# A decoder layer on one core: gate matrices stored in three pieces, and two small loads issued by GpSimd instead of SyncE

## The chip, the cores and the metric

The kernel runs on one core of a Trainium2 chip. The time is device microseconds (us) of one execution, lower is better. The engines are called as the profile calls them: PE (TensorE; PEld is its weight load), DVE (VectorE), ACT (ScalarE), POOL (GpSimd) and SP (SyncE, which only issues DMAs). DMAs issued by SP run on queue q1, those issued by ACT on q10, those issued by POOL on q0; all run on the same 16 DMA engines.

## The reference

One layer on 512 tokens of width 1024: a mixer (Mamba-2 heads beside latent attention), a LayerNorm, and a PEER channel mixer, followed by a last LayerNorm. The change lies in the PEER part, which is, cut to what matters:

```python
q = (xb @ w_query).reshape(T, 8, 2, 128)
s = einsum('thkd,hknd->thkn', q, sub_keys)          # 2 x 128 scores per head
sv, si = top_k(s, 16)
cand_s = sv[:, :, 0, :, None] + sv[:, :, 1, None, :]
top_s, top_pos = top_k(cand_s, 16)                  # 8 heads x 16 experts of 16384
gate = softmax(top_s)
u = take(u_table, expert_idx)                       # rows of 1024
act = gelu(einsum('td,thkd->thk', xb, u))
v = take(v_table, expert_idx)
out = einsum('thk,thkd->td', gate * act, v)
```

## The kernel before, in words

**Tokens.** The 512 tokens are four blocks of 128. Tokens 0 to 335 (`NU`) are done densely: PE multiplies them with the whole table `u` (128 chunks of 128 experts, `u_chunk`), and later a gate-weighted matrix `P` with the whole table `v`. The 48 tokens after them (`UG`, the last of block 2) get their products with `u` by gathering rows (`ug_dots`), and block 3 does both tables by gathering (`gather`).

**Table loads.** `Stream` brings each 512 KB chunk of a table. `loads` issues the load on SP into one of three `wir` buffers (L104), `his` makes the rounded copy `wih` on ACT (L122; every fourth is called `wihx`), `splits` makes the remainder `wil` on DVE, or on POOL while `lo_on` is POOL (L132). A load waits until the subtraction has freed its buffer. A chunk `u_half` is three matmuls for each of eight slices (L85 to L87), and `act_gelu` on ACT empties the accumulator `pu` (L1410, L1411); there are two accumulators.

**Order.** Each engine works through its own list in the order in which the program was written. `drive` interleaves table chunks with another piece of work by estimated durations. After the query projection and the top-16 selection (POOL does the subtractions there) comes `stage2`, which decodes the selected experts of blocks 0 to 2 on DVE (L1054 to L1102); inside it, `ug_index` computes the row numbers of the 48 tokens and sends them by POOL through memory (`ugi`, L1134; `uix`, L1137), and `ug_fetch` gathers rows (`urow`, L1154).

**The inputs of the gathered products.** `UR["x"]` are two tiles in columns of `XT` that are no longer needed. They hold the activations of the 48 tokens, each repeated over partitions: the first has 32 tokens four times, the second 16 tokens eight times (`SETS`). Between the top-16 selection and `stage2` SP loads each with one DMA (L1518), whose source repeats through a step of zero, and whose rows are cut in 16 runs of 64 numbers (256 bytes) by the shape of the tile.

**Gate matrices.** `build_g` then makes, in 48 groups (`n`), the dense gate matrix of blocks 0 to 2. A group is 16 small matmuls (L1291, L1292) and two copies by ACT into `stg` (L1294). Four groups fill one `stg` tile (two alternate), whose store to `gsp[k]` in HBM is one DMA on ACT's queue after the fourth (L1302; L1305 for the last two). Beside this run table chunks, the row gathers and their products (L1160), and, when the buffers for activations are full, stores of activations (`asp<-aout`, L1428, on SP). Then comes the long stage on table `v`, from about 830 us on.

Of the kernel before, what the change touches and what calls it, by code (L numbers as in the profile page):

```python
# [24 lines left out]
D = 1024  # L25
# [6 lines left out]
UG = 48  # L32
SETS = ((16, 32), (0, 16))
NU = NT - UG
ND = NU // 32
NA = ND * 32 + 32
FIRST = 40
KEEP = 51
MORE = 12
# [27 lines left out]
def tile_block(ctx: ExitStack, tc: tile.TileContext, I, out):  # L67
    nc = tc.nc
    ctx.enter_context(tc.manual_schedule())
    V, A, T, G = nc.vector, nc.scalar, nc.tensor, nc.gpsimd  # L70
# [3 lines left out]
    def pool(name, bufs=1, **kw):  # L74
        p = tc.alloc_tile_pool(name=name, bufs=bufs, **kw)
        opened.append(p)
        return p
# [151 lines left out]
    xsp = dram.tile([NB, 128, D], F32, name="xsp")  # L229
    gs0 = dram.tile([128, 2, NT // 32 - ND, 128], F32, name="gs0")  # L230
    gsp = dram.tile([NT // 32, 128, 128, 32], F32, name="gsp")
    acd = dram.tile([64, 128], F32, name="acd")
    ugi = dram.tile([UG, 128], I32, name="ugi")
    asp = dram.tile([PRE - KEEP, 128, NA], F32, name="asp")
    ugg = dram.tile([UG, 128], F32, name="ugg")
# [455 lines left out]
    for n in range(8):  # L691
# [4 lines left out]
        for kk in range(2):  # L696
            k = kp * 2 + kk
# [249 lines left out]
    wide = lambda z: z.rearrange("p (a b) -> p a b", b=64)  # L947
    scl = xt.tile([128, 1], F32, name="scl")
    xt.tile([128, 64], F32, name="edge")
    one16 = xt.tile([128, NA - NU], F32, name="one16")  # L950
    V.memset(one16, 1.0)
# [161 lines left out]
    late = []  # L1113
# [12 lines left out]
    GT, UR = {}, {}  # L1126
    done = []
# [80 lines left out]
    def digits():  # L1208
        dT = ijp.tile([128, 2, 64, 2], F16, name="dT")
        i = GT["ps"][0][:, 2]  # L1210
        x = B1.rearrange("p a b c -> p (a b c)").bitcast(F32)[:, :128].rearrange("p (k c) -> p k c", c=2)
        V.tensor_scalar(x, i, -3.5, BIG, op0=OP.add, op1=OP.add)
        V.tensor_scalar(dT[:, 0], x, -BIG, None, op0=OP.add)
        V.tensor_tensor(dT[:, 1], i, dT[:, 0], op=OP.subtract)
        GT["d"] = dT
# [11 lines left out]
    def build_g():  # L1227
        AT = gb.tile([128, 32, 16, 2], F16, name="tens")
        BT = gb.tile([128, 32, 16, 2], F16, name="units")

        def half(n):
            k0 = n % 16 * 4
            for z, it, w, e in ((AT, iotaE[:, 0:128:8], 16, 0), (B1, iotaE[:, 0:8], 8, 1)):
                b = [128, 32, w, 2]
                V.tensor_tensor(z, it[:, None].to_broadcast(b),
                                GT["d"][:, e, k0:k0 + 32, None].to_broadcast(b), op=OP.is_equal)

        def gates(n, m):
            k = slice(n % 8 * 4, n % 8 * 4 + (m - n) * 4)
            b = [128, (m - n) * 4, 2, 8, 2]  # L1240
            gT = GT[n // 16][1][:, n % 16 * 4:n % 16 * 4 + (m - n) * 4]
            V.tensor_tensor(BT[:, k].rearrange("p k (e i) c -> p k e i c", e=2), B1[:, k, None].to_broadcast(b),
                            gT[:, :, :, None].to_broadcast(b), op=OP.mult)

        def hot(n):
            jT, _, rT = GT[n // 16]
            m = n % 16
            oj = gb.tile([128, 4, 128, 2], F16, name="oj", bufs=2)
            b2 = [128, 4, 128, 2]
            V.tensor_tensor(oj, iotaE[:, None].to_broadcast(b2),  # L1250
                            jT[:, m * 4:m * 4 + 4, None].to_broadcast(b2), op=OP.is_equal)
            g = gb.tile([128, 4, 16, 16, 2], F16, name="g", bufs=2)
            w = 8 if n in LOWA else 16
            b4 = [128, 4, 16, w, 2]
            k = slice(n % 8 * 4, n % 8 * 4 + 4)
            V.tensor_tensor(g[:, :, :, :w], AT[:, k, :, None].to_broadcast(b4),
                            BT[:, k, None, :w].to_broadcast(b4), op=OP.mult)
            for t in range(8 if n in LOWA else 0):
                q, c = divmod(t, 2)
                A.activation(g[:, q, :, 8:, c], g[:, q, :, :8, c], AF.Copy, scale=rT[:, m // 2, q, c:c + 1])  # L1260
            return oj, g

        late = []
        digits()
        g_low()
        half(0)
        gates(0, 8)
        nxt = hot(0)
        dots, head = UR["dots"], ug_head()
        tm[1] += 7.5  # L1270
        yield 2.6
        for n in range(48):
            b, g = divmod(n, 16)
            oj, og = nxt
            lump = 0.0
            if n < 47:
                m = n + 1
                if m % 8 == 0 or m == GG:
                    gates(m, GG if m // 8 == GG // 8 and m < GG else m // 8 * 8 + 8)
                    lump += 0.7  # L1280
                nxt = hot(m)
                if m % 8 == 7 and m < 47:
                    half(m + 1)
                    lump += 1.15
            if g % 4 == 0:
                stg = gs[(n // 4 + 1) % 2].tile([128, 128, 32], F32, name="stg")
            for hf in range(2):
                ps = pw()
                for t in range(4):
                    q, c = hf * 2 + t // 2, t % 2  # L1290
                    T.matmul(ps[:, t * 128:(t + 1) * 128], oj[:, q, :, c], og[:, q, :, :8, c], start=True, stop=False)  # L1291
                    T.matmul(ps[:, t * 128:(t + 1) * 128], oj[:, q, :, c], og[:, q, :, 8:, c], start=False, stop=True)  # L1292
                q0 = g % 4 * 8 + hf * 4
                A.activation(stg[:, :, q0:q0 + 4],  # L1294
                             ps.rearrange("p (t i) -> p i t", t=4), AF.Copy, scale=1.0 / GSC)
            tm[0] += 1.2
            if g % 4 == 3:
                k = n // 4
                if k < ND:
                    done.append(min(FIRST, (un[0] - 2) // 4 * 4))  # L1300
                    late.append((n + 2, k, stg))
                    nc.scalar.dma_start(gsp[k][:, done[k]:], stg[:, done[k]:])  # L1302
                else:
                    nc.scalar.dma_start(gs0[:, :, k - ND], stg[:, 0:8].rearrange("j (q i) t -> j q (i t)", q=2))
                    nc.scalar.dma_start(gsp[k][:, 8:], stg[:, 8:])  # L1305
            if late and late[0][0] <= n:
                _, k, z = late.pop(0)
                acts = ALL[0][:, :done[k], k * 32:k * 32 + 32]
                V.tensor_tensor(acts, acts, z[:, :done[k]], op=OP.mult)
                lump += 0.15 + done[k] * 0.034  # L1310
            if b < 2:
                if g == 9:
                    g_head(b + 1)
                if g == 11:
                    digits()
                    lump += 0.9
                if g == 12:
                    g_low()
                    lump += 1.1
            for _ in range(1 + n % 2):  # L1320
                tm[1] += next(dots, 0.0)
            if 36 <= n <= 40:
                tm[1] += next(head)
            yield lump + (1.45 if n + 1 in LOWA else 1.95) if n < 47 else 0.1
# [43 lines left out]
    aps = [pool("act")]  # L1368
    ALL = [aps[0].tile([128, FIRST, NA], F32, name="acts")]
    out_ = pool("aout")  # L1370
# [7 lines left out]
    def act_tile():  # L1378
# [5 lines left out]
        an[0] += 1  # L1384
        if n < FIRST:
            return ALL[0][:, n]
        return aps[k].tile([128, NA], F32, name="act", bufs=sizes[k] - (0 if k else FIRST))

    def end_tile():
        while an[0] % LEAD < FIRST:  # L1390
            an[0] += 1
        return act_tile().bitcast(F32R)
# [16 lines left out]
    def act_gelu(t, ps):  # L1409
        A.activation(t[:, :NU], ps, AF.Gelu)  # L1410
        A.activation(t[:, NU:], one16, AF.Copy)  # L1411

    def u_half(c, e, psum=None):
# [5 lines left out]
        if e:  # L1419
# [5 lines left out]
            else:  # L1425
                t = out_.tile([128, NA], F32, name="aout", bufs=2)
                act_gelu(t, ps)
# [79 lines left out]
    ug = pool("ug")  # L1507
    UR["x"] = spare(384), spare(448)
    UR["x3"] = UR["x"][0]
    UR["ix"] = ijp.tile([128, UG], I32, name="uix")  # L1510
    UR["hd"] = ijp.tile([128, UG], F32, name="uhd")
    UR["g"] = ijp.tile([UG, 128], F32, name="ugw")
    rt2 = pool("rt2")
    iaE = rt2.tile([128, 16, 16], F16, name="iaE")
    nc.sync.dma_start(iaE.rearrange("p a b -> p (a b)"), I["ch"][:, 256:512])
    for (r, z), x in zip(SETS, UR["x"]):
        d = xsp[2, 128 - UG + r:128 - UG + r + z]
        nc.sync.dma_start(x, bass.AP(tensor=d.tensor, offset=d.offset, ap=[[0, 128 // z], [D, z], [64, 16], [1, 64]]))  # L1518
    lo_on[0] = V
    drive(stage2())  # L1520
    close(rt2)
# [5 lines left out]
    B1 = gb.tile([128, 32, 8, 2], F16, name="unit")  # L1527
    least[0] = 1
    drive(build_g())
    close(gb, *gs)  # L1530
    GS = [-1, 0, 0]
# [91 lines left out]
    def v_prep(c):  # L1623
# [11 lines left out]
        if nb < ND:  # L1635
            A.activation(P[:, nb * 32:ND * 32], a[:, nb * 32:ND * 32], AF.Copy)
        A.activation(P[:, NA:], gt[c // 4][:, ND + 1, c % 4, :], AF.Copy)
        if c % 4 == 3:
# [237 lines left out]
```

## Time and profile before

| | |
|---|---|
| three runs | 1587.13, 1587.03, 1580.26 us |
| median | 1587.03 us |
| profiled execution, its own time | 1587.41 us |
| its span, first to last instruction | 1585.6 us |
| mean granted clock of PE | 0.995 |
| busy in the span: PE, DVE, ACT, POOL | 1552.5, 1345.8, 768.0, 619.2 us |
| moved by DMA | 406.52 MB |

The span is what the profile's rows are counted in; 1.8 us of the execution lie around it. Times at the left of a row are us from the span's start. A row in brackets tells how long the engine stood idle before the instruction and what ended that. A `q` behind an engine's name is its queue, where DMAs are issued.

### The profile page before, as it was taken

What the parts mean: (1) busy time and instruction counts of PE and PEld (TensorE: products, weight loads), DVE (VectorE), ACT (ScalarE), POOL (GpSimd) and SP (SyncE); (2) the same over time, 40 slices, a digit from 0 to 9 for tenths busy, and PEclk for the clock granted to TensorE, in tenths of its full rate; (3) what the DMA queues carried; (4) which work ended last, traced back from release to release, by engine and by line L of the source; (5) the groups of instructions that cost most, each with busy time, mean ns of one, the idle gap of its engine ahead of it and who ended that gap; (6) DMA issues with size and microseconds to landing.
All of it is one profiled execution on the core that took longest, in us unless ns stands there. A gap on an engine that the chain in (4) does not pass through costs nothing.

```text
span 1585.6 us, 24470 instructions
## 1 busy us (share of the span) xinstructions
PE 1552.5 (98%) x8696; PEld 1362.6 (86%) x8696; DVE 1345.8 (85%) x2643; ACT 768.0 (48%) x1539; POOL 619.2 (39%) x443
## 2 busy tenths in 40 slices
PE   9999999999999899999999999999999999999997
PEld 7887888888888899999898999999988878888886
DVE  8978767647799989899976888888889989889997
ACT  5565476731433447676765444443433334344442
POOL 0000032600244224343114655665555556667720
PEclk9999999999999999999999999999999999999999
DMA  6242122474423568899878999999999999999994
GB/s 251 94 160 91 47 75 62 131 236 140 130 81 100 139 220 293 328 337 324 275 249 310 345 360 351 368 355 363 372 336 365 358 360 363 368 341 358 358 314 145
DMA packets 150375, 406.52 MB, mean 256 GB/s; under 512 B 17812, under 2 KB 58980, under 8 KB 148460
## 3 DMA queue, kind: packets, MB, share of 16 engines
q1 hardware_dynamic: 98188, 209.16, 39.2%
q0 software_dynamic: 49648, 176.07, 30.4%
q10 hardware_dynamic: 2416, 19.73, 3.2%
q8 instruction: 68, 1.11, 0.3%
q14 instruction: 55, 0.45, 0.1%
HBM read 374.16 MB, written 28.65 MB: 254 GB/s over the span
## 4 chain that ended last, share of the span: by engine, by line
PE 76%; DMA 8%; DVE 8%; ACT 4%; issue 3%; POOL 0%; DVEq 0%; ACTq 0%; SPq 0%; POOLq 0%
PE va L1677 9%; PE va L1673 9%; PE va L1674 9%; PE pu L85 8%; PE pu L87 8%; PE pu L86 8%; DMA wir<-v 4%; PE pa L86 3%; PE pa L85 3%; PE pa L87 3%; PE pw L86 3%; PE pw L87 3%; PE pw L85 3%; DVE wil L132 2%; DMA wir<-ut 2%
## 5 line engine op out<-in xcount | busy, mean ns | idle before, releaser
L122 ACT ACTIVATE wih<-wir 128x1024 fp32r<-128x1024 f32 (+2 forms) x269 | 277.5, 1032 | 264.7 <-DMA wir<-v 173.7
L132 DVE TENSOR_TENSOR wil<-wir,wih 128x1024 fp32r<-128x1024 f32 (+1 forms) x234 | 282.7, 1210 | 84.3 <-ACT wih L122 59.2
L87 PE MATMUL pu<-XT,wil 128*128 128x336 f32 x1008 | 320.0, 317 | 4.7 <-DVE wil L132 4.3
L1674 PE MATMUL va<-wil,Ph 128*128 128x512 f32 x726 | 282.7, 389 | 0.0
L1554 POOL DMA_INDIRECT row<-v,ix x128 | 222.4, 1738 | 133.3 <-DVE ac L1571 108.7
L1673 PE MATMUL va<-wih,Ph 128*128 128x512 f32 x624 | 243.4, 390 | 0.0
L1554 POOL DMA_INDIRECT row<-u,ix x128 | 187.2, 1463 | 134.2 <-DVE row L1565 97.6
L85 PE MATMUL pu<-XT,wih 128*128 128x336 f32 x648 | 208.0, 321 | 1.0 <-ACT acts L1410 1.0
L86 PE MATMUL pu<-XT,wih 128*128 128x336 f32 x648 | 204.8, 316 | 0.0
L87 PEld LDWEIGHTS pu<-XT,wil 128*128 128x128 f32 x1008 | 190.5, 189 | 6.2 <-DVE wil L132 5.4
L1677 PE MATMUL va<-wih,Pl 128*128 128x512 f32 x624 | 192.9, 390 | 1.1 <-DVE Pl L1664 1.1
L1571 DVE SCALAR_TENSOR_TENSOR ac<-row,hd,ac 128x1024 f32<-128x1024 f32 x128 | 164.0, 1281 | 8.1 <-DMA row<-v,ix 6.3
L1565 DVE SCALAR_TENSOR_TENSOR row<-row,XT 128x1024 f32<-128x1024 f32 x128 | 150.7, 1221 | 10.1 <-DMA row<-u,ix 10.0
L1674 PEld LDWEIGHTS va<-wil,Ph 128*128 128x128 f32 x726 | 136.3, 188 | 26.6
L1677 PEld LDWEIGHTS va<-wih,Pl 128*128 128x128 f32 x624 | 117.0, 188 | 26.7 <-DVE Pl L1664 1.9
L1673 PEld LDWEIGHTS va<-wih,Ph 128*128 128x128 f32 x624 | 117.2, 188 | 22.7
L132 POOL TENSOR_TENSOR wil<-wir,wih 128x1024 fp32r<-128x1024 f32 (+3 forms) x35 | 73.0, 2093 | 154.3 <-PE pw L87 99.2
L85 PEld LDWEIGHTS pu<-XT,wih 128*128 128x128 f32 x648 | 122.2, 189 | 2.7 <-ACT acts L1410 1.4
L86 PEld LDWEIGHTS pu<-XT,wih 128*128 128x128 f32 x648 | 122.4, 189 | 1.1
L85 PE MATMUL pu<-XT,wihx 128*128 128x336 f32 x360 | 115.7, 322 | 6.3 <-ACT acts L1410 6.3
L1154 POOL DMA_INDIRECT urow<-u,uix x48 | 72.8, 1518 | 114.4 <-DVE urow L1160 102.7
L86 PE MATMUL pu<-XT,wihx 128*128 128x336 f32 x360 | 114.3, 317 | 0.0
(519 smaller groups left out, 3294.0 us busy)
## 6 DMA issues: line engine op xcount, KB each, us to landing
wir<-ut SPq DMA_DIRECT2D x128, 512.0 KB
wir<-v SPq DMA_DIRECT2D x128, 512.0 KB
gt<-gsp SPq DMA_DIRECT2D x22, 768.0 KB
wir<-wo SPq DMA_DIRECT2D x26, 512.0 KB
wir<-wf SPq DMA_DIRECT2D x18, 512.0 KB
gsp<-stg ACTq DMA_DIRECT2D x6, 1408.0 KB
wir<-wqr SPq DMA_DIRECT2D x16, 512.0 KB
de<-acd POOLq DMA_DIRECT2D x8, 512.0 KB
```

What stands on the lines that cost most here:

```text
L85: T.matmul(ps, lh, rh, start=start, stop=False)
L86: T.matmul(ps, lh, rl, start=False, stop=False)
L87: T.matmul(ps, ll, rh, start=False, stop=stop)
L122: A.activation(h, r, AF.Copy)
L132: self.lo(n).tensor_tensor(l, r, h, op=OP.subtract)
L1154: G.indirect_dma_start(out=UR[n], out_offset=None, in_=I["u"], in_offset=bass.IndirectOffsetOnAxis(ap=UR["ix"][:, n:n + 1], axis=0))
L1554: G.indirect_dma_start(out=R[s], out_offset=None, in_=I["u"] if s < 128 else I["v"], in_offset=bass.IndirectOffsetOnAxis(ap=ix[:, s % 128: ...
L1565: V.scalar_tensor_tensor(wide(r), wide(r), 1.0, x3, op0=OP.mult, op1=OP.mult, accum_out=hd[:, s:s + 1])
L1571: V.scalar_tensor_tensor(ac, r, hd[:, s - 128:s - 127], ac, op0=OP.mult, op1=OP.add)
L1673: T.matmul(va[b][e], Ph[b], h[:, cs], start=c == 0, stop=False)
L1674: T.matmul(va[b][e], Ph[b], l[:, cs], start=False, stop=False)
L1677: T.matmul(va[b][e], Pl[b], h[:, cs], start=False, stop=c == 127)
```

## The change

The two loads of `UR["x"]` leave SP. POOL issues them as twelve DMAs, four of 32 tokens and eight of 16 tokens, each one copy to one group of partitions, ahead of the tiles that follow. The store of a gate matrix is cut in three (`PIECES`) along the columns; one piece is issued at the end of each group, so the second and third go out one and two groups later. In the last group all that is left is issued at once. The two small stores to `gs0` stay as they are.

```diff
+PIECES = 3
...
-        late = []
+        late, stores = [], []
...
                     late.append((n + 2, k, stg))
-                    nc.scalar.dma_start(gsp[k][:, done[k]:], stg[:, done[k]:])
+                    e = [done[k] + (128 - done[k]) * x // PIECES for x in range(PIECES + 1)]
+                    stores.extend((gsp[k][:, x:y], stg[:, x:y]) for x, y in zip(e, e[1:]))
                 else:
                     nc.scalar.dma_start(gs0[:, :, k - ND], stg[:, 0:8].rearrange("j (q i) t -> j q (i t)", q=2))
-                    nc.scalar.dma_start(gsp[k][:, 8:], stg[:, 8:])
+                    e = [8 + 120 * x // PIECES for x in range(PIECES + 1)]
+                    stores.extend((gsp[k][:, x:y], stg[:, x:y]) for x, y in zip(e, e[1:]))
+            while stores:
+                nc.scalar.dma_start(*stores.pop(0))
+                if n < 47:
+                    break
...
     UR["x"] = spare(384), spare(448)
     UR["x3"] = UR["x"][0]
+    for (r, z), x in zip(SETS, UR["x"]):
+        for i in range(128 // z):
+            G.dma_start(x[i * z:(i + 1) * z], wide(xsp[2, 128 - UG + r:128 - UG + r + z]))
...
-    for (r, z), x in zip(SETS, UR["x"]):
-        d = xsp[2, 128 - UG + r:128 - UG + r + z]
-        nc.sync.dma_start(x, bass.AP(tensor=d.tensor, offset=d.offset, ap=[[0, 128 // z], [D, z], [64, 16], [1, 64]]))
```

The order of instructions on PE and DVE is the same in both kernels; line numbers are higher by 1 from the new constant on, by 7 behind the stores, and by 10 between the place of the new loads and that of the old. What stands on SP around the moved loads, `wir<-ut` being loads of table `u`; before:

```order
L104 DMA wir<-wqr 128x1024 x4
L1458 DMA SK<-skT 128x512
L104 DMA wir<-wqr 128x1024
L104 DMA wir<-ut 128x1024 x10
L1515 DMA iaE<-ch 128x256
L1518 DMA XT<-xsp 128x16x64 x2
L104 DMA wir<-ut 128x1024 x45
```

and after:

```order
L105 DMA wir<-wqr 128x1024 x4
L1465 DMA SK<-skT 128x512
L105 DMA wir<-wqr 128x1024
L105 DMA wir<-ut 128x1024 x10
L1525 DMA iaE<-ch 128x256
L105 DMA wir<-ut 128x1024 x45
```

The two loads no longer stand between the tenth and the eleventh table load. On POOL, at its last subtractions ahead of `stage2` and the row numbers behind them; before:

```order
L132 TENSOR_TENSOR wil<-wir,wih 128x1024 x3
L132 TENSOR_TENSOR wil<-wir,wihx 128x1024
L132 TENSOR_TENSOR wil<-wir,wih 128x1024
L1134 DMA ugi<-p_5497 48x128
L1135 DMA ugg<-ijg 48x128
```

and after:

```order
L133 TENSOR_TENSOR wil<-wir,wih 128x1024 x3
L133 TENSOR_TENSOR wil<-wir,wihx 128x1024
L133 TENSOR_TENSOR wil<-wir,wih 128x1024
L1519 DMA XT<-xsp 32x16x64 x4
L1519 DMA XT<-xsp 16x16x64 x8
L1135 DMA ugi<-p_5507 48x128
L1136 DMA ugg<-ijg 48x128
```

Twelve loads now stand between the last subtraction and the row numbers. On ACT, from the store of the first four groups of `build_g` to the copies that end the sixth; before:

```order
L1302 DMA gsp<-stg 128x3456
L122 ACTIVATE wihx<-wir 128x1024
L1410 ACTIVATE acts<-pu 128x336
L1411 ACTIVATE acts<-one_3369 128x16
L1294 ACTIVATE stg<-pw 128x128x4 x2
L122 ACTIVATE wih<-wir 128x1024
L1410 ACTIVATE acts<-pu 128x336
L1411 ACTIVATE acts<-one_3369 128x16
L1260 ACTIVATE g<-g,rT 128x16x8 x8
L1294 ACTIVATE stg<-pw 128x128x4 x2
```

and after:

```order
L1310 DMA gsp<-stg 128x1152
L123 ACTIVATE wihx<-wir 128x1024
L1417 ACTIVATE acts<-pu 128x336
L1418 ACTIVATE acts<-one_3369 128x16
L1295 ACTIVATE stg<-pw 128x128x4 x2
L1310 DMA gsp<-stg 128x1152
L123 ACTIVATE wih<-wir 128x1024
L1417 ACTIVATE acts<-pu 128x336
L1418 ACTIVATE acts<-one_3369 128x16
L1261 ACTIVATE g<-g,rT 128x16x8 x8
L1295 ACTIVATE stg<-pw 128x128x4 x2
L1310 DMA gsp<-stg 128x1152
```

The first piece goes out where the whole store did; the second and third stand behind the copies of the next two groups.

## The prediction

> **What bounds the kernel now.** I read the page first (busy shares, the chain), then the busy time by stretch, then the stretches in which TensorE (PE) falls short, and there each engine's timeline, the chain and the DMA queues.
>
> ```profile
> PE 1552.5 (98%) x8696; PEld 1362.6 (86%) x8696; DVE 1345.8 (85%) x2643; ACT 768.0 (48%) x1539; POOL 619.2 (39%) x443
> PE 76%; DMA 8%; DVE 8%; ACT 4%; issue 3%; POOL 0%; DVEq 0%; ACTq 0%; SPq 0%; POOLq 0%
> ```
>
> PE is the bound: it is busy 98% of the span and has 76% of the chain. Only a stretch in which PE stands still, or runs at a lower clock, can be won. The windows show where that is (us, then busy time and instruction count by engine, granted clock, DMA share, GB/s):
>
> ```profile
> core 0: us, PE busy (x) PEld busy (x) DVE busy (x) ACT busy (x) POOL busy (x), PEclk, DMA share, GB/s
> 530.00:540.00 10.00, 10.00 (x67) 10.00 (x66) 9.75 (x30) 6.56 (x11) 0.15 (x1) 1.00 0.43 100
> 540.00:550.00 10.00, 5.90 (x39) 5.62 (x37) 8.38 (x8) 0.83 (x3) 0.00 (x0) 0.99 0.79 186
> 550.00:560.00 10.00, 7.84 (x38) 7.84 (x39) 8.20 (x7) 6.01 (x12) 2.93 (x5) 0.67 0.48 150
> 660.00:680.00 20.00, 18.88 (x127) 17.77 (x125) 18.19 (x25) 13.93 (x35) 8.00 (x6) 0.91 0.83 299
> 760.00:780.00 20.00, 16.89 (x167) 15.88 (x167) 19.96 (x27) 12.92 (x30) 6.47 (x10) 1.00 0.85 274
> ...
> 592.00:815.00 223.00, 217.54 (x1852) 209.68 (x1851) 205.85 (x280) 156.32 (x373) 74.14 (x58) 0.99 0.84 300
> 860.00:1290.00 430.00, 425.28 (x2283) 383.63 (x2282) 368.83 (x536) 177.02 (x354) 247.78 (x173) 1.00 0.97 355
> ```
>
> There are two places. From 540 to 560 PE issues 39+38 matmuls where 67 fit into 10 us: 57 are missing, at 6.7 per us a loss of **8.5 us**, a stall and a half clock behind it. In the stretch of the gate matrices (592 to 815) PE lacks 223.00-217.54 = 5.5 us, and at 660 to 680 the clock of 0.91 means 3.6 us at half speed, 1.8 us more: **7.3 us**. Together 15.8 us, 1.0% of the time. From 860 on PE is 98.9% busy, so what is won earlier is kept, though the DMA engines are at 0.97.
>
> The first place: SP's timeline (start, length, what it issued), the one step of the chain there, and the timelines of ScalarE (ACT) and PE, with the idle time before a row and what ended it in brackets:
>
> ```profile
> 531.03 9.58 SPq L1518 DMA_DIRECT2D XT<-xsp  x2
> 540.72 196.30 SPq L104 DMA_DIRECT2D wir<-ut  x45
> ...
> 540.72 9.91 DMA wir<-ut
> ...
> 550.71 1.06 ACT L122 ACTIVATE wih<-wir 128x1024 fp32r<-128x1024 f32 x1 [9.88 <-DMA wir<-ut]
> 551.67 0.43 ACT L1410 ACTIVATE acts<-pu 128x336 f32<-128x336 f32 x1
> 552.16 0.65 PE L85 MATMUL pu<-XT,wihx 128*128 128x336 f32 x1 [6.26 <-ACT acts L1410]
> ```
>
> SP spends 9.58 us on the two `XT` loads; the next table load goes out at 540.72 and needs 9.91 us. ScalarE waits 9.88 us for it, with the GELU of a finished chunk (L1410) behind that wait, and PE waits 6.26 us for the GELU to free its accumulator. The DMA queues (packets, MB, share of the 16 engines) from 534 to 544, and from 770.5 to 773, when the same kind of load, issued by GpSimd at 768.30 (L1166), was moved:
>
> ```profile
> q1 hardware_dynamic: 3094, 0.79, 39.8%
> ...
> q0 software_dynamic: 157, 0.50, 75.2%
> ```
>
> From SP the load is packets of 0.79 MB/3094 = 256 bytes, 0.79 MB in 10 us. From GpSimd the same pattern went in 157 packets, 0.50 MB in 2.5 us.
>
> **The change part by part.** *The `XT` loads leave SP.* The table load of 540.72 needs only its buffer, which the subtraction at 536.06 frees. The timelines' rows for a table load on free queues, for VectorE (DVE) and for GpSimd (POOL):
>
> ```profile
> 586.38 0.33 SPq L104 DMA_DIRECT2D wir<-ut  x1
> 590.17 1.06 ACT L122 ACTIVATE wihx<-wir 128x1024 fp32r<-128x1024 f32 x1 [1.68 <-DMA wir<-ut]
> ...
> 536.06 1.22 DVE L132 TENSOR_TENSOR wil<-wir,wih 128x1024 fp32r<-128x1024 f32 x1
> 544.95 1.22 DVE L132 TENSOR_TENSOR wil<-wir,wihx 128x1024 fp32r<-128x1024 f32 x1
> 548.52 0.42 DVE L1102 TENSOR_TENSOR ijg<-eq 128x256 f32<-128x256 f16 x1
> 551.80 1.22 DVE L132 TENSOR_TENSOR wil<-wir,wih 128x1024 fp32r<-128x1024 f32 x1 [2.86 <-ACT wih L122]
> ...
> 527.73 2.42 POOL L132 TENSOR_TENSOR wil<-wir,wih 128x1024 fp32r<-128x1024 f32 x1 [1.26 <-PE pu L87]
> 553.52 0.54 POOL L1134 DMA_DIRECT2D ugi<-p  x1 [23.37 <-DVE p L1133]
> 768.30 1.20 POOL L1166 DMA_DIRECT2D XT<-xsp  x1
> 773.75 3.30 POOL L1404 DMA_DIRECT2D act<-asp  x6
> ```
>
> So it can go out at 537.3. On free queues such a load lands in 590.17-586.38 = 3.8 us, beside the `XT` packets in 9.91; the faster form of L1166 is the nearer to free queues, and I take 5 us: landed at 542.3, L122 done by 543.4, the GELU by 543.9, before PE runs out (552.16-6.26 = 545.9). The wait for the accumulator goes. Next late is VectorE: the subtraction of 544.95 ends at 546.2, 0.3 us late; a chunk is 24 matmuls, 24/6.7 = 3.6 us, so PE wants the following one at 549.8; the subtraction of 551.80 moves up by its 2.86 us of waiting to 548.94 and ends at 550.2, 0.4 us late. Gain 8.5-0.7 = **7.8 us**. Its lower end is the 5.6 of the first rival, its upper end 8.5.
>
> GpSimd issues twelve loads instead. Nearest rows: 0.55 us (L1404, one run of memory per partition) to 1.20 us (L1166, 2048 runs); with 512 and 256 runs I take 0.7 and 0.63 us, 4x0.7+8x0.63 = 7.8 us, bounds 6.6 to 14.4. They start when the last subtraction ends (530.15) and stand ahead of `ugi`, which waits 23.37 us until 553.5; that wait hides them, even at 14.4. With the cover gone, `ugi`, the row gathers and the dot products would come as much later.
>
> *The gate stores in pieces.* Twelve stores become 36. The DMA queues from 644 to 653 without a store and from 654 to 662 with one; steps of the chain; the waits of 592 to 815 (total, times, longest); and what an issue costs ScalarE (min/median/max ns):
>
> ```profile
> q0 software_dynamic: 383, 1.40, 38.8%
> q1 hardware_dynamic: 292, 1.06, 38.0%
> ...
> q10 hardware_dynamic: 144, 1.64, 62.4%
> q0 software_dynamic: 161, 0.60, 18.5%
> q1 hardware_dynamic: 87, 0.36, 10.9%
> ...
> 654.61 8.87 DMA wir<-ut
> 741.40 0.33 ACTq L1302
> 742.36 8.69 DMA asp<-aout
> ...
> DVE wil L132 <- ACT wih L122: 7.1, 4, 2.7
> PE pw L1291 <- DVE g L1256: 4.1, 4, 2.1
> L1302 ACTq DMA_DIRECT2D gsp<-stg x10: 326/326/357, 610.3 to 788.1; - x10
> L1305 ACTq DMA_DIRECT2D gsp<-stg x2: 619/620/622, 801.6 to 812.8; - x2
> ```
>
> From 644 to 653 the table loads (q1) have 38.0% of the DMA engines. From 654 to 662 one store, 128 packets of 12.8 KB, takes 62.4% and leaves q1 10.9%; the table load of 654.61 needs 8.87 us, and PE loses 1.1 us and the half clock (2.9 in all). The store of 741.40 does the same to `asp` (8.69 us): ScalarE waits for that buffer, VectorE comes late by up to 2.7 us (the longest of its four waits), and VectorE, 99.8% busy from 760 to 780, then makes PE wait 3.1 us. A piece has 3.7 to 5.1 KB per partition, near the loads' 4 KB, so three queues share about evenly: 512 KB at a third of 300 GB/s is 5 us, not 8.9. I take the 2.9 us whole and 2.0 of the 3.1, since VectorE has no slack of its own there, and leave the rest of the 7.3: **4.9 us**, bounds 0 to 7.3. New cost: 24 more issues, 20x0.326+4x0.62 = 9.0 us of ScalarE, which is busy 156.32 of 223; hidden, so 0, with 9.0 if that cover were gone. What waits: the third piece goes out two groups later, the buffer is written again three groups after that, 14 us at 223/48 = 4.6 us a group, against about 6 us to land. In the last group three pieces stand ahead of L122 on ScalarE, 1.2 us more there, in a stretch without a PE stall: 0 to 1.2.
>
> The Trainium skill's page "DMA: Bandwidth & Descriptors", section "Rules for kernel authors", asks for at least 1 MiB per DMA and speaks against this cut. Its fit (fixed 2.0 us plus bytes over 436 GB/s, section "Anatomy of one DMA — SWDGE (gpsimd) path") makes an estimate of 3 x 3.1 us for three pieces against 5.3 us for one store, which no engine waits for; by it the sum is the same.
>
> **Sum**, against the profiled execution (1587.41 us; 0.4 above the median of 1587.03): 1587.4-7.8-4.9 = 1574.7, so **1575 us**.
>
> **Rivals.** *Moving the queue saves only SP's issue time.* The same bytes on the same engines might hold the table load as long: issued 3.4 us earlier and 9.91 us under way it lands at 547.2, the GELU is done at 548.8, and PE stands from 545.9 on for 2.9 us; the 3.1 us idle at 760 to 780 left the clock at 1.00, so without a half clock: 8.5-2.9 = 5.6 gained; with the stores 1577. For it: q1 took every byte slowly at 534 to 544. Against: the 2.5 us of L1166. The Trainium skill's page "DMA: Bandwidth & Descriptors", section "Rules for kernel authors", says that spreading DMAs over issuers saves only issue time; by that rule this is the outcome, and the L1166 row disagrees with it for this pattern.
>
> *The stores' pieces bring nothing*, because VectorE (205.85 of 223) sets the pace of that stretch: 1587.4-7.8 = 1579.6. For it: 99.8% busy from 760 to 780. Against: its 7.1 us of waits on ScalarE are the loads' lateness.
>
> *Slower: a store always in flight.* Pieces a group apart keep all three queues loaded, and each table load lands later. 45 loads in 196.30 us are one per 4.36 us; with three buffers a load may take 13.1 us in all, of which ScalarE and VectorE need 1.06+1.22 and about 1.5 of queueing, so it decides at a mean landing of 9.3 us. At 11 us each of some 45 loads costs 1.7/3 us, 25 us; 1587.4-7.8+25 = 1605. Against: 8.87 us was reached with 12.8 KB packets only.
>
> *The cover fails and nothing is won* (row gathers late behind twelve issues, or the gain eaten by VectorE): 1584 to 1590.
>
> **Chances.** Both gains 0.52, only issue time 0.12, no store gain 0.18, nothing 0.11, slower 0.07. The range 1568 to 1584 holds the first three with their bounds (1587.4-8.5-7.3 = 1571.6, and 3 us for runs that differ) and leaves some 0.2 out. A difference under 0.5% (7.9 us, below 1579.1) can't be told from none: faster 0.52+0.10+0.05 = 0.67; same 0.25; slower 0.08.
>
> **What would show it.** SP's row at 531 gone and no PE idle over 1 us between 540 and 556, clock 1.00 at 550 to 560; packets under 512 B fewer by about 4096; GpSimd's twelve issues ended by 540, `ugi` near 550; q10 under 40% in any 8 us between 600 and 800; PE idle at 592 to 815 under 3 us. I am wrong if table loads there take over 9 us on the mean, if ScalarE's wait for `wir` grows, or if VectorE is 99% busy from 545 to 600 with PE waiting for it.

## The result, and the profile after

| | before | changed |
|---|---|---|
| median of the first comparison (7 runs each) | 1586.47 us | 1574.32 us (1570.51 to 1578.96) |
| median of a second one, on another chip (35 and 12 runs) | 1585.40 us | 1575.46 us (1573.00 to 1582.88) |
| profiled execution, its span | 1587.41, 1585.6 us | 1574.32, 1572.6 us |

The ratio of the times is 0.9941 (95% interval 0.9923 to 0.9960) in the first comparison and 0.9947 (0.9929 to 0.9965) in the second: faster by 0.5 to 0.6%, 8 to 9 us. The forecast was 1575.

The same windows of the changed kernel from 540 to 815 us (busy time and instructions by engine, granted clock, DMA share, GB/s):

```profile
core 0: us, PE busy (x) PEld busy (x) DVE busy (x) ACT busy (x) POOL busy (x), PEclk, DMA share, GB/s
540.00:550.00 10.00, 9.97 (x65) 9.59 (x63) 9.44 (x9) 4.88 (x12) 0.00 (x0) 1.00 0.50 145
550.00:560.00 10.00, 10.00 (x66) 9.85 (x65) 9.90 (x11) 5.01 (x11) 3.56 (x6) 1.00 0.58 166
660.00:680.00 20.00, 20.00 (x161) 19.55 (x160) 18.42 (x27) 14.20 (x35) 7.10 (x5) 1.00 0.86 310
760.00:780.00 20.00, 19.74 (x196) 18.70 (x195) 19.86 (x28) 16.85 (x39) 4.36 (x8) 1.00 0.85 289
592.00:815.00 223.00, 220.45 (x1874) 214.24 (x1873) 208.93 (x294) 161.65 (x382) 76.02 (x62) 1.00 0.88 312
```

The page's line of busy times is led by PE as before:

```profile
PE 1546.8 (98%) x8696; PEld 1358.0 (86%) x8696; DVE 1346.1 (86%) x2643; ACT 767.9 (49%) x1539; POOL 622.8 (40%) x455
```

From 540 to 560 PE now issues 65+66 matmuls at full clock where it issued 39+38. In the stretch of the gate matrices its idle time is 223.00-220.45 = 2.55 us (5.46 before), and the clock is 1.00 at 660 to 680. In a second profile of the changed kernel, from the comparison on the other chip, that idle time is 223.00-218.06 = 4.94 us, hardly less than before. More than half of it is one stall, behind a table load that was 7.65 us under way:

```profile
716.49 0.23 PE L1292 MATMUL pw<-g,oj 128*128 128x128 f16 x1 [2.91 <-DVE g L1257]
```

The rows behind the first place: the timelines of SP, ACT, DVE and POOL.

```profile
537.46 3.03 SPq L105 DMA_DIRECT2D wir<-ut  x2
542.76 1.06 ACT L123 ACTIVATE wih<-wir 128x1024 fp32r<-128x1024 f32 x1 [1.94 <-DMA wir<-ut]
548.88 1.22 DVE L133 TENSOR_TENSOR wil<-wir,wih 128x1024 fp32r<-128x1024 f32 x1
530.08 6.09 POOL L1519 DMA_DIRECT2D XT<-xsp  x9
538.42 0.56 POOL L1519 DMA_DIRECT2D XT<-xsp  x1 [0.34 <-DMA XT<-xsp]
550.59 0.53 POOL L1135 DMA_DIRECT2D ugi<-p  x1 [11.61 <-DVE p L1134]
```

The table load goes out at 537.46 and ACT has it at 542.76 (forecast 537.3 and 542.3). POOL's twelve issues end at 538.98, and `ugi` still waits 11.61 us behind them for VectorE: the cover held.

One stall is new. The chain of work that ended last, from 567 to 583 (start, length, what), and PE's row at its end:

```profile
567.64 6.04 DMA wir<-ut
...
573.76 1.06 ACT wih L123
574.82 0.16 ACT jT L1204
574.98 0.18 ACT gT L1205
...
575.18 0.30 DVE unit L1213
...
579.89 0.46 DVE g L1257
580.35 0.68 issue
581.02 1.23 DVE wil L133
```

```profile
582.30 0.42 PE L88 MATMUL pu<-XT,wil 128*128 128x336 f32 x1 [2.08 <-DVE wil L133]
```

A table load is 6.04 us under way; ACT's cast of it stands ahead of the two copies `jT` and `gT`, VectorE starts on the gate matrices only then, and its next subtraction, 5.8 us later, is late for PE.

To see where time is won, the n-th of the 8696 matmuls of a kernel can be set against the n-th of the kernel before: the order is the same, so the difference of their starts is the lead there. Places are named by the time in the profile before. The table has all kernels of this study, with the median of their runs and the ratio to the kernel before on the same chip.

| kernel | lead at 556 | 592 | 680 | 815 | 1100 us | median | ratio (95%) |
|---|---|---|---|---|---|---|---|
| changed, first profile | 7.9 | 5.6 | 9.9 | 11.8 | 11.4 | 1574.32 | 0.9941 (0.9923 to 0.9960) |
| changed, second profile | 8.1 | 6.7 | 10.8 | 10.2 | 10.0 | 1575.46 | 0.9947 (0.9929 to 0.9965) |
| `XT` loads by POOL alone | 7.9 | 5.5 | 9.2 | 8.8 | 8.7 | 1580.59 | 0.9977 (0.9959 to 0.9995) |
| twelve `XT` loads by SP alone | 8.1 | 6.8 | 10.4 | 9.9 | 10.0 | 1580.06 | 0.9971 (0.9950 to 0.9992) |
| six `XT` loads by SP, zero step of two | -15.4 | -15.7 | -12.4 | -13.7 | -13.7 | 1603.01 | 1.0109 (1.0077 to 1.0141) |
| pieces alone | 1.5 | 0.7 | 5.1 | 7.1 | 6.2 | 1581.80 | 0.9977 (0.9957 to 0.9997) |
| changed, pieces at once by ACT | 8.0 | 3.1 | 6.8 | 1.0 | 0.4 | 1588.18 | 1.0020 (1.0003 to 1.0037) |
| changed, pieces at once by SP | 7.8 | 7.0 | 8.6 | 5.6 | 5.7 | 1584.34 | 0.9986 (0.9963 to 1.0008) |
| changed, four pieces | 8.1 | 6.3 | 10.5 | 10.4 | 7.0 | 1581.38 | 0.9980 (0.9961 to 0.9999) |
| changed, two subtractions on POOL | 8.0 | 4.4 | 8.8 | 10.7 | 10.0 | 1577.22 | 0.9950 (0.9929 to 0.9970) |
| changed, a dot product later | 7.5 | 4.6 | 4.2 | 6.1 | 5.0 | 1583.66 | 0.9992 (0.9970 to 1.0015) |
| changed, transposes earlier | 7.8 | 7.0 | 11.2 | 13.1 | 12.4 | 1574.05 | 0.9922 (0.9896 to 0.9949) |
| the same, twelve loads by SP | 8.0 | 7.2 | 11.5 | 13.4 | 12.4 | 1575.94 | 0.9948 (0.9926 to 0.9971) |

The lead is that of one execution. Single times of one kernel scatter by up to 9 us to either side, and behind 1100 us leads drift by up to 6.5; so small differences are read from the places, and only the intervals count for the times.

### The profile page after: what moved, and what is told of

It reads as the page before. It is cut to its first block, busy times and chain, and to the rows that moved or that the text cites. A ratio compares the mean times of both kernels' runs of the same rounds, so it can differ in the third digit from the quotient of the medians.

```text
span 1572.6 us, 24526 instructions
## 1 busy us (share of the span) xinstructions
PE 1546.8 (98%) x8696; PEld 1358.0 (86%) x8696; DVE 1346.1 (86%) x2643; ACT 767.9 (49%) x1539; POOL 622.8 (40%) x455
## 4 chain that ended last, share of the span: by engine, by line
PE 75%; DVE 10%; DMA 7%; issue 4%; ACT 3%; POOL 1%; DVEq 0%; ACTq 0%; POOLq 0%
PE va L1684 9%; PE va L1681 9%; PE va L1680 9%; PE pu L86 8%; PE pu L88 8%; PE pu L87 8%; DMA wir<-v 4%; PE pa L87 3%; PE pa L86 3%; PE pa L88 3%; PE pw L87 3%; PE pw L88 3%; PE pw L86 3%; DVE wil L133 2%; DMA wir<-ut 2%
## 5 line engine op out<-in xcount | busy, mean ns | idle before, releaser
L1561 POOL DMA_INDIRECT row<-v,ix x128 | 217.5, 1699 | 136.6 <-DVE ac L1578 114.7
L123 ACT ACTIVATE wihx<-wir 128x1024 fp32r<-128x1024 f32 x67 | 70.9, 1058 | 91.8 <-DMA wir<-ut 55.6
L1663 ACT ACTIVATE Ph<-P 128x384 fp32r<-128x384 f32 x121 | 62.7, 518 | 107.5 <-DVE P L1640 90.2
## 6 DMA issues: line engine op xcount, KB each, us to landing
gt<-gsp SPq DMA_DIRECT2D x22, 768.0 KB, 10.2
```

What stands on the lines that cost most here:

```text
L123: A.activation(h, r, AF.Copy)
L1561: G.indirect_dma_start(out=R[s], out_offset=None, in_=I["u"] if s < 128 else I["v"], in_offset=bass.IndirectOffsetOnAxis(ap=ix[:, s % 128: ...
```

## Experiments

### Each half alone

*Only the `XT` loads:* the kernel before with

```diff
+            G.dma_start(x[i * z:(i + 1) * z], wide(xsp[2, 128 - UG + r:128 - UG + r + z]))
...
-        nc.sync.dma_start(x, bass.AP(tensor=d.tensor, offset=d.offset, ap=[[0, 128 // z], [D, z], [64, 16], [1, 64]]))
```

> Only the XT loads are moved to GpSimd, in twelve copies; the gate stores stay whole. Theory A (the two places add up): TensorE is 8.0 us ahead of the kernel before at 556 us, loses 2.4 of it at about 580, where VectorE is late, and keeps 5.6 to the end: about 1580.9 us against 1586.5. Theory B (the 8.0 us are kept here, and it is the pieces that cost 2.4 at 580): 1578.5. Theory C (what is won at the first place is eaten in the stretch of the whole stores, since VectorE has no slack there): under 2 us won, 1584.5 or more.

*Only the pieces:* the changed kernel with the two loads of the kernel before back on SP.

> Only the gate stores are cut in three pieces; the XT loads stay with SyncE. Theory A (the two places add up): 6.2 us won between 660 and 770 and up to 0.9 behind it, 1579.4 to 1580.3 us against 1586.5. By the sum on record it would be 4.9, 1581.6. Theory B (the pieces help only where TensorE comes 5.6 us earlier to that stretch): under 2 us, 1584.5 or more.

*The changed kernel again:*

> The changed kernel again, as a base on the same chip as the other kernels of this set. Theory A (the two places add up, the rest is scatter of the long stage): 9 to 13 us under the kernel before; TensorE 7.9 us ahead at 556, 5.5 to 8 at 592 and 11 to 12 at 815. Theory B (the gain of 12 us was mostly the luck of a profile): under 7 us.

Leads of 7.9 and 5.5 at 556 and 592 for the loads alone, and 7.1-0.7 = 6.4 from 592 to 815 for the pieces alone: by places, theory A in both. The time of the pieces alone, 1581.80 us, lies between their two theories. The changed kernel again is 9.9 us below the kernel before, as its theory A has it, but 10.2 us ahead at 815 and not 11 to 12. The sum of the halves does not hold from 592 to 815, though. The loads alone, with whole stores, also win 8.8-5.5 = 3.3 us in that stretch, mostly near 667, where the kernel before lost an idle microsecond and a half clock. That loss is missing with either half. In its second profile the changed kernel wins no more than that, 10.2-6.7 = 3.5 us, since the stall shown above takes 2.9 us back. What the pieces have to themselves is at 762 to 768, 2.3 to 2.8 us in both profiles of the changed kernel and in that of the pieces alone, against 0.6 with whole stores. ACT's wait for the buffer that `asp` empties, between 592 and 815 (total, times, longest), with the loads alone and with the pieces alone:

```profile
ACT aout L1410 <- DMA asp<-aout: 4.9, 1, 4.9
```

```profile
ACT aout L1417 <- DMA asp<-aout: 2.2, 1, 2.2
```

It was 5.5 before and is 2.3 in the changed kernel (in its second profile 4.3 in two waits, the longest 2.7). By the ratios the times say 0.23% for each half and 0.53 to 0.59% for both: they add up within the intervals, some 3.6 us each, with 1 to 2 us open.

### Who issues the loads, and in which form

*Twelve loads by SP:* the kernel before, and at the place of its two loads

```diff
-        nc.sync.dma_start(x, bass.AP(tensor=d.tensor, offset=d.offset, ap=[[0, 128 // z], [D, z], [64, 16], [1, 64]]))
+        for i in range(128 // z):
+            nc.sync.dma_start(x[i * z:(i + 1) * z], wide(xsp[2, 128 - UG + r:128 - UG + r + z]))
```

> The kernel before, with one thing altered: SyncE issues the XT loads at their old place, but as the same twelve copies without the zero step. Packets, bytes and the order on SyncE stay. Theory A (SyncE's issue time, 9.6 us, and its 256-byte packets hold the next table load): the load goes out at 540 or later and lands at 550; TensorE waits 4 to 6 us; nothing won at 556. Theory B (the zero step of the source kept the two loads on few of the DMA engines, and that made the table load slow): the load goes out at 540.7, lands in 5 us at 546, and TensorE is 6 us ahead at 556, as with GpSimd.

*Six loads by SP, each with a zero step:*

```diff
+        for i in range(0, 128, 2 * z):
+            nc.sync.dma_start(x[i:i + 2 * z], bass.AP(tensor=d.tensor, offset=d.offset, ap=[[0, 2], [D, z], [64, 16], [1, 64]]))
```

> The kernel before, but SyncE issues the XT loads as six, each with a zero step of two copies (two of 64 partitions, four of 32), in place of two with zero steps of four and eight. Bytes, packets and place stay. Theory A (a zero step of c copies keeps a load on about c of the 16 DMA engines, and that is what makes the table load behind it slow): the loads are spread no better, the DMA share stays at 0.1 to 0.6 from 533 to 547, TensorE still waits 4 us or more near 545 and nothing is won at 556. Theory B (few large DMAs instead of many small ones was the fault): half of the gain of twelve copies or more, TensorE 4 to 8 us ahead at 556.

Theory B in the first; in the second A, and worse than A had it, since 15.4 us are lost at 556 where A expected nothing to be won. SP's timeline with twelve loads, and ACT's cast of the table load behind them:

```profile
530.93 8.59 SPq L1518 DMA_DIRECT2D XT<-xsp  x12
539.62 1.02 SPq L104 DMA_DIRECT2D wir<-ut  x2
...
543.75 1.06 ACT L122 ACTIVATE wih<-wir 128x1024 fp32r<-128x1024 f32 x1 [3.02 <-DMA wir<-ut]
```

SP is as busy as before (8.59 against 9.58 us), the packets are the same 256 bytes, and still PE is 8.1 us ahead at 556. What differs is how many DMA engines work on the loads. The DMA share in 40 equal slices, in tenths, what moved (GB/s), and SP's queue (packets, MB, share): the kernel before from 534 to 544, twelve loads from 534 to 541, six loads from 530 to 560.

```profile
DMA  3333336333333333333333333333333466666676
GB/s 73 73 73 66 61 72 117 46 48 58 67 54 47 48 68 71 67 59 73 73 68 66 73 72 55 60 73 74 71 79 88 95 143 145 146 139 128 142 103 97
```

```profile
DMA  9999999999999999879965001682274236606826
...
q1 hardware_dynamic: 3635, 0.90, 83.2%
```

```profile
DMA  0768411211111111112111111111111111111111
GB/s 0 76 213 339 157 36 37 44 22 27 31 29 33 35 34 35 33 36 47 36 35 36 36 36 36 32 36 37 36 36 33 36 36 37 37 36 36 36 37 36
```

A source that repeats four times through a zero step keeps 0.3 of the engines busy, eight times 0.6, twice 0.1; without a zero step all of them. The rates follow the copies: 36 GB/s with two, 73 with four, 145 with eight. With six loads SP is held for 28.04 us by issuing them, the table load behind them goes out only at 559.25, and PE stands:

```profile
531.11 28.04 SPq L1519 DMA_DIRECT2D XT<-xsp  x6
...
567.60 0.65 PE L85 MATMUL pu<-XT,wihx 128*128 128x336 f32 x1 [21.62 <-ACT acts L1410]
```

1603.01 us, 1.1% slower than before, with three times as many and smaller DMAs. So what delayed the table load in the kernel before is neither that SP issues the loads (issuing twelve takes it 8.59 us, and PE does not wait), nor the size of the packets, nor that they are two large DMAs, but the leading zero step. In these runs the zero step is also the source's outermost dimension, of size 2, 4 or 8; no run has such a small outermost dimension without a repeat, so the two are not told apart. The Trainium skill, "DMA: Bandwidth & Descriptors", section "Rules for kernel authors", says this: an outermost dimension of size c below 16, "e.g. a leading zero-stride broadcast of c copies", confines the DMA to at most c engines. The rates agree, in proportion to c; the shares of 0.1, 0.3 and 0.6 are near 2, 4 and 8 of 16 (0.125, 0.25, 0.5), the last two a little above, which no run here explains.

### The pieces: how many, and when

*Issued at once:* the changed kernel without

```diff
-                if n < 47:
-                    break
```

> As the changed kernel, but the three pieces of a store are issued one behind the other at once, after the fourth group. Theory A (the size of a packet decides: 3.7 to 5.1 KB a partition instead of 12.8 KB lets the table loads pass): TensorE idle 2.5 to 3.5 us between 592 and 815, time within 1.5 us of the changed kernel's 1574.3. Theory B (the spreading in time decides: three pieces at once fill the queue as long as one store): table loads of 8 to 11 us, the stalls near 667 and 765 come back, 5 to 6 us, 1579.5 to 1580.5.

*At once, by SP:* in addition

```diff
-                nc.scalar.dma_start(*stores.pop(0))
+                nc.sync.dma_start(*stores.pop(0))
```

> As the run with the three pieces issued at once, but SyncE issues them, not ScalarE (also those of the last groups). Theory A (with the pieces at once it is ScalarE's time for three issues in a row, 1.5 to 2.3 us ahead of the cast of a table chunk, that makes VectorE and then TensorE late): ScalarE's waits named issue ahead of its casts, 10.9 us, fall under 4, TensorE's idle time from 592 to 815 falls from 8.9 to 2.5 to 5 us, and the time comes to within 3 us of the changed kernel. Theory B (the three pieces in flight together are the fault): TensorE idle 7 us or more, 1585 us or more.

*Four pieces:* `PIECES = 4`.

> As the changed kernel, with four pieces in place of three, so that a piece goes out at the end of every group and a store is always in flight. Theory A (spread pieces cost only issues that are hidden on ScalarE): within 1.5 us of the changed kernel, TensorE idle 2.5 to 3.5 us between 592 and 815. Theory B (a store always in flight makes each table load later, the slower rival on record): table loads of over 9 us on the mean there, 10 to 25 us longer.

Issued at once by ACT, the pieces lose all that they bring, and more (1588.18 us): theory B by its outcome, and in part by its reason. At 762 to 768 no more is won than with whole stores (0.5 us against 0.6), and ACT's wait for the buffer that `asp` empties is 5.3 us again, as long as with whole stores (6.1 with SP as issuer): there it is the spreading in time that helps. The late table loads of theory B are not seen. ACT's waits for them are shorter than in the changed kernel (6.3 against 12.8 us), and by the traces' records of landings, some of which are missing, those issued between 592 and 815 are 6.0 us under way on the mean (6.0 in the changed kernel, 6.4 before). What is longer is ACT's own issuing. The waits of that kernel from 592 to 815, and one such place in the timelines of ACT and PE:

```profile
DVE wil L133 <- ACT wih L123: 16.4, 7, 3.7
ACT wih L123 <- issue: 10.9, 5, 2.4
PE pw L1292 <- DVE g L1257: 8.1, 5, 3.3
ACT wih L123 <- DMA wir<-ut: 6.3, 3, 3.3
```

```profile
715.94 2.32 ACTq L1310 DMA_DIRECT2D gsp<-stg  x3
718.30 1.06 ACT L123 ACTIVATE wih<-wir 128x1024 fp32r<-128x1024 f32 x1 [2.39 <-issue]
...
722.41 0.23 PE L1292 MATMUL pw<-g,oj 128*128 128x128 f16 x1 [3.28 <-DVE g L1257]
```

Three issues in a row take 1.5 to 2.3 us instead of 3 x 0.33, right ahead of the cast of a table chunk; VectorE waits for the cast (16.4 us in all, 7.8 and 9.4 in the two profiles of the changed kernel), the one-hot products come late, and PE waits. Part of that run's loss lies ahead of any store: 4.9 us near 580, a stall of 2.49 with a low clock behind it (0.88 on the mean of 578 to 592). With SP as issuer ACT's waits on issuing go, as theory A has it, but PE is still idle 223.00-215.73 = 7.27 us, as theory B has it: ACT now waits more often for table loads, which stand behind the pieces on SP (total, times, longest).

```profile
ACT wih L123 <- DMA wir<-ut: 17.9, 10, 5.1
```

In the changed kernel these waits are 12.8 and 17.3 us, six each. By the same records the table loads are 6.7 us under way on the mean, and eight of them over 9 us (with ACT as issuer one). So three issues in a row delay what stands behind them on ACT, and on SP the table loads that follow them are later. Beside three pieces in flight together the `asp` store is as long under way as beside a whole store (8.52 us, 8.69 before); that pieces issued by ACT hold the table loads of SP is not seen.

Four pieces are neither of the two theories: the table loads were not later on the whole (ACT waits 9.8 us for `wih`, less than 12.8), so a store always in flight did them no harm; but the time is 1581.38 us, some 6 above the changed kernel. Up to 815 the lead is the same; the last group then issues what is left at once, ACT waits 4.3 us on it ahead of one cast (2.3 and 3.0 us with three pieces), and 3.4 us of lead are gone by 1100. That this explains all 6 us is not shown.

### The stall at 580

Three attempts on the changed kernel, and the last of them once more with SP as issuer of the loads; all have the same order on PE but for the early transposes.

*Two subtractions on POOL:*

```diff
+    sub_g = [win.ns + x for x in (2, 3)]
+    win.lo = lambda n: G if n in sub_g else lo_on[0]
```

> As the changed kernel, but two of the subtractions of table chunks (the third and fourth behind the switch to VectorE) are done by GpSimd, behind its twelve loads and ahead of the row numbers. Theory A (VectorE is the bound from 546 to 582, and its work makes TensorE stand 2.24 us at 580): VectorE is some 2.4 us earlier from 550 on, the stall at 580 falls below 0.5 us, 1572.3 us. Theory B (the table load of 573.83, 6.44 us under way beside the row gathers, makes that stall): the stall stays at 1.5 us or more, 1574.3 us.

*A dot product later:* `yield next(UR["dots"])` ahead of `g_head(0)` becomes `yield 1.2`, and the dot product is done in the fourth group of `build_g`.

> As the changed kernel, but VectorE's first dot product of a gathered row (1.22 us, at 571.44) is done five groups later. Theory A (VectorE's work, not a transfer, makes TensorE stand 2.24 us at 580): the stall falls to about 1.0 us, TensorE 6.8 us ahead of the kernel before at 592 and not 5.6; 1.2 us off the time. Theory B (the table load of 573.83 makes that stall): it stays 2 us or more, and the time too.

*Transposes earlier:* `g_head(0)` is called ahead of the last two steps of the decoding.

> As the changed kernel, but the three transposes that open the gate matrices, and ScalarE's two copies of them, are written one step of the decoding earlier, ahead of the cast of the table chunk that ScalarE waits for at 573. Theory A (the stall at 580 comes from the table load of 567.6, late beside the row gathers: ScalarE's copies stand behind its cast, VectorE waits 1.37 us for them and its 5.9 us of work ahead of the subtraction starts late): VectorE's wait of 1.4 us for gT is gone, the stall falls by 1.4 us to 0 to 0.9, up to 1.5 us off the time, which the times can hardly tell. Theory B (VectorE's work alone): wait gone, but the stall stays, since VectorE is then busy with something else.

*The same with the twelve loads issued by SP:*

> As the run before this one (early transposes, stores in pieces), but the twelve copies are issued by SyncE at the place of the old loads, and none by GpSimd. Theory A (it is the form of the loads and not the issuer): within 2 us of the run before this, TensorE 8 us ahead of the kernel before at 556. Theory B (GpSimd's issuing is worth something of its own, since SyncE has the table loads to issue): 2 to 5 us slower than the run before this, the table load behind the copies at 543.7 and not 542.7.

The first missed: the stall at 580 is gone, but stalls of 1.86 and 1.49 us at 553 and 570 took its place, since VectorE was not relieved. Its timeline and POOL's:

```profile
538.93 3.53 DVE L133 TENSOR_TENSOR wil<-wir,wih 128x1024 fp32r<-128x1024 f32 x1
545.11 3.96 DVE L1097 TENSOR_TENSOR eq<-eq,tif 128x4096 f16<-128x4096 f16 x1 [0.46 <-DVE eq L1093]
```

```profile
538.95 2.42 POOL L133 TENSOR_TENSOR wil<-wir,wihx 128x1024 fp32r<-128x1024 f32 x1
543.25 3.68 POOL L133 TENSOR_TENSOR wil<-wir,wih 128x1024 fp32r<-128x1024 f32 x1 [1.88 <-ACT wih L123]
```

A subtraction of 1.22 us on VectorE takes 3.53 beside one of 2.42 on POOL, and the 2.29 us of L1097 become 3.96: two subtractions saved (2.4 us) cost 2.3+1.7 us. The Trainium skill, "SBUF — State Buffer", section "SBUF: two separate sides", describes the port pair that VectorE and GpSimd share as an exclusive lock held for a whole instruction, also when VectorE's operation has two inputs in SBUF and GpSimd's reads SBUF; 1.22+2.42 = 3.64 against 3.53 agrees.

The dot product missed too: VectorE was free 1.2 us earlier and waited for `gT` instead; the stall was 2.50 us, behind a table load (of 568.01) that took 6.67 us. In the second profile of the changed kernel that load took 4.72 us, and the stall was 0.25 with 0.55 at 568. So the size of the stall goes with that load, by way of ACT's order. The 4.8 us that this kernel lost near 630 were not followed up.

Early transposes did what theory A said. ACT's copy, and VectorE's first step and its subtraction:

```profile
569.66 0.28 ACT L1206 ACTIVATE gT<-px 128x128 f16<-128x128 f32 x1
...
573.83 0.28 DVE L1214 TENSOR_SCALAR unit<-px 128x128 f32<-128x128 f32 x1
...
579.68 3.49 DVE L133 TENSOR_TENSOR wil<-wir,wih 128x1024 fp32r<-128x1024 f32 x3
```

The 1.37 us of waiting are gone, the subtraction starts 1.3 us earlier, and no stall is left at 580 (0.57 us at 568; with the loads on SP 0.54 at 580). How much of that the edit did is not shown: the table load was quicker there too (5.47 and 4.90 us for 6.04), and the second profile of the changed kernel has next to no stall at 580 without the edit. Both kernels have the largest leads at 815, 13.1 and 13.4. Their times, 1574.05 and 1575.94, can't be told from the changed kernel's. That the second, which issues nothing more on POOL, is as good within the intervals is one more sign that the issuer does not matter.

## Why the prediction was right, point by point

The time (1575) and its range held, and so did the direction; the working behind them held in part.

- **The first place, 7.8 us.** Measured 7.5 to 8.1 at 556 in every kernel without a zero step. The steps at the load, the cast and the GELU were right to 0.5 us, POOL's issues ended at 538.98 (540), `ugi` came at 550.59 (550).
- **Its reason was wrong.** The step failed that took the speed of the row at L1166 for a property of GpSimd's queue. It was the zero step that was missing there. The rival on record, that moving a queue saves only issue time, was right as a rule (SP does as well with twelve loads); its time, 1577, was wrong because the change does not only move the queue. The row at L1166 does not speak against the rule either, since that load has no zero step. That the 7.8 us came is luck as far as the working goes: the new loads also left out the zero step, and the prediction did not count on that.
- **"Next late is VectorE": the search stopped at 550.** The 0.3+0.4 us there were not seen, but 2.4 and 1.4 us went at 568 to 581 in the two profiles of the changed kernel, and 0.8 to 5.0 in the others with the gain. The row gathers came 6.6 us earlier (559.35 for 565.93) and met the table loads just where PE had come 8 us nearer to VectorE. That term was missing in the sum: the loads alone end at 3.8 to 5.3 us by the medians.
- **The pieces, 4.9 us.** Mis-sized: the 2.9 us at 660 to 680 do not need the pieces. With whole stores the loads alone and the twelve loads by SP also pass that place without the low clock. The 2.0 at 760 to 780 were low (2.3 to 2.8), and 0.6 of that comes without pieces. The pieces on their own are worth about 3.6 us by the ratio of the times. The 5 us taken for a table load beside a piece were 6.0 on the mean of all table loads there.
- **"Hidden" issues on ACT.** Right for 0.33 us a group, and only so: issued three in a row they cost PE several microseconds. The last group's extra cost was put at 0 to 1.2 us; ACT's wait there is 2.3 and 3.0 us in the two profiles, 1.0 and 1.7 above the 1.3 of before, without a stall of PE there.
- **The base.** 1587.41 us was a long execution; the medians of before in five sets are 1584.37 to 1586.47. The sum of 7.8+4.9 = 12.7 us was too large (8 to 9 by the ratios, 9.9 and 12.2 by the medians) and started 1 to 3 us too high; the two errors cancel in 1575.
- **The slower rival** (a store always in flight) is not borne out by four pieces, where loads were not later. Two of the signs listed missed: q10 had 40 to 44% in four 8 us windows and 53% in the last one, not under 40; packets under 512 bytes are 3532 fewer, not 4096. Two more came out as listed in the first profile of the changed kernel and not in the second: PE's idle time from 592 to 815 is 4.94 us there, not under 3, and ACT's wait for table loads, one of the signs of being wrong, is 17.3+2.7 = 20.0 us there, against 16.3+1.3 = 17.6 before and 12.8+2.6 = 15.4 in the first. So the pieces do not keep the table loads early in every execution.

## What to carry to other kernels

Look at the DMA share while a load is alone on its queue: 0.1, 0.3 or 0.6 that stays level was a load on a few engines here, and what had to change was the leading zero step of its source, not the queue that issues it. A long store is cut best where its pieces can go out one at a time between other work of the issuing engine. When a stall is taken away, follow the engine that is next late until its next free time, here 30 us on, not only to the next chunk.

## What the runs showed of the hardware that was not expected

- A leading zero step of few copies in the source holds a DMA to a rate in proportion to the copies, some 18 GB/s each with 256-byte packets (36, 73 and 145 GB/s with two, four and eight).
- VectorE and GpSimd hold each other up in operations on two tensors (a subtraction of 1.22 us on VectorE becomes 3.53, one of 2.42 on GpSimd 3.68).
- ACT's third DMA issue in a row takes 0.5 to 1.5 us instead of 0.33 where the pieces are issued at once.
- The clock's fall does not follow the length of a stall: after 1.05 us of idle PE at 667 in the kernel before it fell (0.76 on the mean of 666 to 673), and after two stalls of 2.08 and 2.91 us, at 580 in the changed kernel and at 713 in its second profile, it did not. What else decides it is not shown here.
